# Up-projection weight sums moved from VectorE to GpSimd, read from a second copy of the weight, and two layouts in DRAM changed

## The chip, the cores and the metric

One core of a Trainium2 chip runs the whole program. The metric is the device time of one execution in microseconds (us). The engines are named as in the profile: PE is TensorE (with PEld, its weight loads), DVE is VectorE, ACT is ScalarE, POOL is GpSimd, and SP is SyncE, which does nothing here but issue DMAs, one after the other, from one queue in program order.

## What is computed

One layer of a streaming encoder over 2048 prompt tokens and 64 sample tokens, all in float32: a modulated RMSNorm, one input projection that feeds a pooling mixer and an mLSTM with 4 heads, an output projection, then a second modulated norm and a gated MLP with a causal convolution of width 3. The part that the change touches belongs to the MLP:

```
up = h2 @ w_up                      # (tokens, 1024) @ (1024, 5632)
conv = b_conv + sum(w_conv[j] * upp[:, j:j + T] for j in range(3))
a, g = split(conv, 2)
x = x + gt2 * ((silu(g) * a) @ w_down)
```

## The kernel before

**Number format.** A float32 matrix product is made of three passes: each operand is kept as a high part and a low part (ACT copies to the high part, line 411; DVE subtracts to get the low one, line 414; together a "split"), and high x high, high x low and low x high are added in PSUM. A split weight block is a tile `wt` of 128 partitions x 2 x 512; there are 7 such buffers. A block that comes unsplit from DRAM lands in a `raw` tile first.

**Stages.** Attention runs in 4 groups g of 512 tokens (the last one of 576), up to about 800 us of the span. In each, PE walks through the projections (line 1117 for `v`, line 477 for q, k, the output gate, the pooling input and the output projection). The mLSTM of a head is made of small pieces of work between these matmuls: `GL` (a copy of decays from PSUM to SBUF on DVE), `kw` (the keys times decays, DVE, from PE's transposes on line 1282), the state update `st`, `SP` (DVE, from PE's line 1307), the outputs `nd` (DVE), and a scale `sf` and a row scale `RS`, whose power of -0.5 POOL takes (lines 1349 and 545). The MLP then runs in 3 groups of 704 tokens (line 1572 is the up-projection).

**Up-projection with seven products.** The weight of the up-projection is cut into 22 blocks f. Per block, Strassen's scheme needs 7 products: three of them (lines of `up_unit`) use pieces of `w_up` itself, the other four (`sum_unit`) use sums and differences of its four pieces a0, a1, g0, g1. These four sums are worked out while attention groups 1 to 3 run, by the generator `up_sums` (lines 843 to 872), and kept in DRAM (`wsum`). There are 44 items: 22 blocks times two halves of 256 columns. An item is a load of a tile `w` (4 x 256 columns, two DMAs, four buffers `w4`), four additions or subtractions on DVE (lines 863, 864, 866, 867), and a store. Loads are made three items ahead. The generator is moved on by one step at four places of each projection row (`tick(4)` in `gemm`), and its instructions are pinned to keep their order among themselves. The MLP's first group reads all four sums from `wsum`, splits them and keeps three of them split in `wsplit`; the later two groups read those three split and the fourth from `wsum` again.

**Kept split weights.** In attention group 0 the q, k, gate and pooling weights are split once and kept in DRAM (`hl_kept`, 32 blocks, line 419 stores), and groups 1 to 3 load them from there (line 395). Their last axis is 528 long, of which 512 are used.

**Another user of DVE and SP.** In groups 1 to 3 the generator `ada` makes more modulation vectors: for 16 steps i = 0 to 15, a load of `raw` from `w_ada` (line 194) and two multiply-adds on DVE (line 210; line 208 for the first of each half). These too sit in DVE's and SP's order between the other work.

**What sets the order.** A scheduler orders each engine's instructions at build time, and on the chip every engine runs its list in order. Waits are on semaphores, so an instruction that waits holds back all behind it on its engine or queue. A DMA also waits for the one eight places before it, which used the same semaphore. A `w4` buffer can be loaded again only when the store from it has landed.

Of the kernel before, what the change touches and what calls it, by code (L numbers as in the profile page):

```python
# [9 lines left out]
F32 = mybir.dt.float32  # L10
F32R = mybir.dt.float32r
AF = mybir.ActivationFunctionType
ALU = mybir.AluOpType
# [3 lines left out]
P = 128  # L17
D = 1024
KD = D // P
# [5 lines left out]
NF = 22  # L25
# [17 lines left out]
WN = 2 * 264  # L43
# [19 lines left out]

@with_exitstack
def tile_layer(ctx: ExitStack, tc: tile.TileContext, xT, vecs, cst, rst, w_mod, w_ada, w_qkou, w_v, w_pool,
               w_out, w_up, w_down, w_quad, st_C, st_pool, yT, o_pool, o_C, o_m, o_conv):
    nc = tc.nc
    act, dve, pool, pe = nc.scalar, nc.vector, nc.gpsimd, nc.tensor

# [12 lines left out]
    dr = ctx.enter_context(tc.tile_pool(name="dr", bufs=1, space=DRAM))  # L82
# [17 lines left out]
    def scr():  # L100
        return sp.tile([P, TMAX], F32, tag="scr", name="scr")


    bg = ([], [], [], [], [])
# [152 lines left out]
    for g in range(NG):  # L257
# [20 lines left out]
    OUT, INSIDE, WHOLE = range(3)  # L278
    stream = []

    hl_kept = dr.tile([32, P, 2, WN], F32, tag="hl_kept", name="hl_kept")
    place_of = {}

    def halves(key, src, n):
# [39 lines left out]

    def sum_unit(g, f, i):
        if i not in KEPT:
            return (wsum[f, :, i], 512, INSIDE, None)
        kept = wsplit[f, KEPT.index(i)]
        return (kept, 512, WHOLE, None) if g else (wsum[f, :, i], 512, INSIDE, kept)

    dsum = dr.tile([8, P, 4, 512], F32, tag="dsum", name="dsum")

    def quad_units(p, first):

        out = []
        for d in (2 * p, 2 * p + 1):
            raw, sums = [[(t[d, :, i], 512, place, None) for i in range(4)] for t, place in ((w_quad, OUT), (dsum, INSIDE))]
# [35 lines left out]
    class Unit:  # L373

        state = 0
        w = raw = None
# [7 lines left out]
    def issue():  # L384
        u = Unit()
        src, u.n, place, u.keep, u.stays = stream[pos[0]] + (OUT, None, False)[len(stream[pos[0]]) - 2:]
        u.at = pos[0]
        if place == OUT:
            u.raw = raw_tile()
            nc.sync.dma_start(out=u.raw[:, :u.n], in_=src)  # L390
        else:
            u.w = wt_tile(u.n)
            if place == WHOLE:
                u.state = 2
                nc.sync.dma_start(out=u.w.bitcast(F32)[:, :, :u.n], in_=src)
            else:
                u.raw = u.w.bitcast(F32)[:, 1]
                nc.sync.dma_start(out=u.raw[:, :u.n], in_=src)
        pos[0] += 1
        pend.append(u)  # L400

# [269 lines left out]
    class Sums:  # L671
# [165 lines left out]
    if True:  # L837
# [3 lines left out]
        C = a1.tile([P, NCST], F32, tag="C", name="C")  # L841
        RST = a1.tile([4, TMAX], F32, tag="RST", name="RST")

        def up_sums():

            def load(f, c):
                w = a1.tile([P, 4, 256], F32, tag="w4", name="w4", bufs=4)
                for i in range(2):
                    tc.keep_in_program_order(nc.sync.dma_start(out=w[:, 2 * i:2 * i + 2, :], in_=w_up[NF * i + f].rearrange(
                        "p (h c) -> p h c", h=2)[:, :, c:c + 256]))  # L850
                return w
            todo = [(f, c) for f in range(NF) for c in (0, 256)]
            pin = tc.keep_in_program_order
            nx = [load(*todo[i]) for i in range(3)]
            yield
            yield
            for i, (f, c) in enumerate(todo):
                w = nx.pop(0)
                yield
                yield  # L860

                a0, a1_, g0, g1 = (w[:, i, :] for i in range(4))
                pin(dve.tensor_tensor(out=g1, in0=g0, in1=g1, op=ALU.add))
# [3 lines left out]
                pin(dve.tensor_tensor(out=a1_, in0=a1_, in1=a0, op=ALU.subtract))  # L867
                yield

                if i + 3 < len(todo):  # L870
                    nx.append(load(*todo[i + 3]))
                pin(nc.sync.dma_start(out=wsum[f, :, :, c:c + 256], in_=w))

        def fold():

# [92 lines left out]
        h, pb, pr0 = [], [], []  # L968
# [462 lines left out]
        for o in groups:  # L1431
            drain(1)
            if o.g == 1:
                bg[4].append(up_sums())
            if o.g > 0:
                bg[3].append(ada(2 + o.g, False))
            if o.g == 0:
# [10 lines left out]
            if o.g == 0:  # L1448
                t = scr()
# [11 lines left out]
            for hd in range(NH):  # L1461
# [38 lines left out]
            h = hn  # L1500
# [14 lines left out]
    todo = []  # L1515
# [149 lines left out]
    class Pair:  # L1665
# [115 lines left out]
        def blocks(self):  # L1781
            return [self.of(i)[:, j * FH:(j + 1) * FH] for i in range(1 + self.second) for j in (0, 1)]
# [306 lines left out]
    for o in fgroups:  # L2089
        Bo = B[o.g]  # L2090
        held = None
        for pi, part in enumerate(PARTS[o.g]):
# [99 lines left out]
            for secs in [(c,) for c in ENDS] if ends else (ENDS,):  # L2192
                sums = [(ssum, 0)]
# [98 lines left out]
```

## Time and profile before

| what | value |
|---|---|
| time, median of 3 runs | 2187.92 us (2184.07 to 2188.07) |
| span of the profiled execution, first to last instruction | 2178.0 us |
| between the median and that span | 9.92 us |
| PE busy in the span | 2155.1 us (99%) |
| DVE busy | 1631.7 us (75%) |
| ACT busy | 1093.7 us (50%) |
| POOL busy | 241.6 us (11%) |
| moved by DMA | 539.51 MB in 297351 packets |

The time of the profiled execution itself is not listed beside its span; the runs listed differ from the span by what lies around the first and the last instruction, and the prediction takes that part as unchanged. "Busy" counts an engine's instructions while they run; for PE the ends of matmuls are modelled, so short waits can hide inside them. A row of a group of instructions has line, engine, operation, output and inputs, shapes, the count, then the busy time, the mean duration of one in ns, and the idle time just before them with what ended it. A timeline row has start, length, engine, line and tile, and in brackets the idle time before it and what ended that.

### The profile page before, as it was taken

The numbers are of one execution on the slowest core, as the hardware profiler recorded it, in microseconds if no ns is written. First come the engines' busy times: TensorE is split into PE (matmuls) and PEld (weight loads), VectorE is DVE, ScalarE is ACT, GpSimd is POOL, SyncE is SP. The second block draws the span as 40 slices with busy tenths as digits, with TensorE's granted clock in tenths as the row PEclk, the third lists the DMA queues.
The fourth block names the chain that finished last, engine by engine and source line by source line (L and its number), as shares of the span: only waits on it lengthen the run. The fifth ranks groups of instructions, "written<-read, shape, count | busy, mean of one in ns | idle before, by whom it ended". The sixth has DMA issues, their size and how long they took to land.

```text
span 2178.0 us, 38112 instructions
## 1 busy us (share of the span) xinstructions
PE 2155.1 (99%) x13553; PEld 2041.6 (94%) x13553; DVE 1631.7 (75%) x3040; ACT 1093.7 (50%) x2181; POOL 241.6 (11%) x474
## 2 busy tenths in 40 slices
PE   8999999999999999999999999999999999999998
PEld 7888888888899999999999999999999999999998
DVE  5868668757955678797967668888886587887874
ACT  4554335234333456474736445655655364565554
POOL 0010000001000101010101121100101331111112
PEclk9999999999999999999999999999999999999999
DMA  8886997988879387788967966666668675555542
GB/s 325 327 297 226 312 312 259 310 291 273 296 263 305 130 279 255 267 306 295 349 211 257 316 244 225 237 201 215 227 220 275 217 255 183 170 179 190 172 161 81
DMA packets 297351, 539.51 MB, mean 248 GB/s; under 512 B 25760, under 2 KB 114336, under 8 KB 297160
## 3 DMA queue, kind: packets, MB, share of 16 engines
q1 hardware_dynamic: 287720, 514.75, 69.8%
q10 hardware_dynamic: 9440, 22.32, 2.6%
q8 instruction: 107, 1.75, 0.3%
q14 instruction: 84, 0.69, 0.1%
HBM read 410.98 MB, written 125.98 MB: 247 GB/s over the span
## 4 chain that ended last, share of the span: by engine, by line
PE 82%; DMA 7%; DVE 7%; issue 2%; ACT 1%; SPq 1%; POOL 0%; DVEq 0%; POOLq 0%; ACTq 0%
PE mm L1572 35%; PE mm L477 19%; PE mm L2138 12%; PE mm L2015 8%; PE mm L1117 2%; DVE wt L414 2%; DMA raw<-w_ada 1%; DMA wt<-wsum 1%; DMA hl_kept<-wt 1%; DMA wsum<-w 1%; PE m L1307 1%; PE m L1329 1%; PE m L1327 1%; PE m L1292 1%; DVE scr L250 1%
## 5 line engine op out<-in xcount | busy, mean ns | idle before, releaser
L1572 PE MATMUL mm<-hx,wt 128*128 128x352 f32 x5544 | 887.0, 321 | 3.7 <-DVE hx L768 1.9
L1572 PEld LDWEIGHTS mm<-hx,wt 128*128 128x128 f32 x5544 | 878.6, 188 | 6.8 <-DVE hx L768 2.8
L477 PE MATMUL mm<-hl,wt 128*128 128x512 f32 (+2 forms) x1920 | 386.2, 357 | 0.2 <-ACT va L250 0.2
L411 ACT ACTIVATE wt<-raw 128x512 fp32r<-128x512 f32 (+3 forms) x470 | 276.8, 597 | 185.2 <-PE mm L477 63.5
L477 PEld LDWEIGHTS mm<-hl,wt 128*128 128x128 f32 x1920 | 315.4, 189 | 48.2 <-issue 5.3
L414 DVE TENSOR_TENSOR wt<-raw,wt 128x512 fp32r<-128x512 f32 (+3 forms) x470 | 312.2, 670 | 53.2 <-ACT wt L411 52.7
L2138 PE MATMUL mm<-av,wt 128*128 128x448 f32 (+1 forms) x1632 | 262.7, 322 | 0.0
L2138 PEld LDWEIGHTS mm<-av,wt 128*128 128x128 f32 x1632 | 250.4, 188 | 11.1
L1987 DVE SCALAR_TENSOR_TENSOR x<-mm,MOD,x 128x352 f32<-128x352 f32 (+3 forms) x360 | 167.2, 503 | 79.2 <-PE mm L2138 65.7
L2015 PE MATMUL mm<-av,wt 128*128 128x352 f32 x1344 | 220.6, 323 | 1.8 <-DVE x L1987 0.7
L2015 PEld LDWEIGHTS mm<-av,wt 128*128 128x128 f32 x1344 | 215.4, 188 | 4.8 <-DVE ea L1581 2.8
L1619 ACT ACTIVATE mm<-mm 128x352 f32<-128x352 f32 x196 | 87.8, 448 | 240.0 <-PE mm L1572 184.0
L477 PE MATMUL mm<-mx,wt 128*128 128x512 f32 (+1 forms) x960 | 182.6, 352 | 0.0
L477 PEld LDWEIGHTS mm<-mx,wt 128*128 128x128 f32 x960 | 159.3, 188 | 22.5
L1550 DVE SCALAR_TENSOR_TENSOR ta<-ea,V,ta 128x704 f32<-128x704 f32 (+1 forms) x132 | 125.6, 952 | 63.2 <-ACT ta L1545 51.2
L1550 DVE SCALAR_TENSOR_TENSOR tg<-eg,V,tg 128x704 f32<-128x704 f32 (+1 forms) x132 | 125.7, 952 | 61.0 <-ACT tg L1545 58.5
L414 DVE TENSOR_TENSOR wt<-wt 128x512 fp32r<-128x512 f32 x196 | 132.7, 683 | 12.8 <-ACT wt L411 12.7
L411 ACT ACTIVATE wt<-wt 128x512 fp32r<-128x512 f32 x196 | 119.2, 622 | 43.1 <-DMA wt<-wsum 40.1
L1759 ACT ACTIVATE tg<-tg 128x704 f32<-128x704 f32 (+1 forms) x66 | 52.5, 795 | 70.5 <-DVE tg L1550 70.5
L1528 POOL COPY ea<-UC 128x2 f32<-128x2 f32 x66 | 32.8, 497 | 482.6 <-DVE ta L1550 394.0
L1117 PE MATMUL mm<-wt,hl 128*128 128x256 f32 (+1 forms) x576 | 71.3, 284 | 0.0
L1117 PEld LDWEIGHTS mm<-wt,hl 128*128 128x128 f32 x576 | 70.4, 190 | 0.8 <-issue 0.6
(304 smaller groups left out, 2188.2 us busy)
## 6 DMA issues: line engine op xcount, KB each, us to landing
wt<-wsplit SPq DMA_DIRECT2D x132, 512.0 KB, 4.2
raw<-w_up SPq DMA_DIRECT2D x198, 256.0 KB, 3.8
wt<-hl_kept SPq DMA_DIRECT2D x96, 512.0 KB, 6.0
wt<-wsum SPq DMA_DIRECT2D x132, 256.0 KB, 5.3
wsplit<-wt SPq DMA_DIRECT2D x66, 512.0 KB, 5.5
w<-w_up SPq DMA_DIRECT2D x88, 256.0 KB, 3.7
wsum<-w SPq DMA_DIRECT2D x44, 512.0 KB, 4.9
Bd<-fscr ACTq DMA_DIRECT2D x56, 352.0 KB, 4.3
```

The costliest lines, as they stand in the source:

```text
L411: act.activation(u.w[:, 0, :u.n], u.raw[:, :u.n], AF.Copy)
L414: dve.tensor_tensor(out=u.w[:, 1, :u.n], in0=u.raw[:, :u.n], in1=u.w[:, 0, :u.n].bitcast(F32), op=ALU.subtract)
L477: pe.matmul(ps[bi][:, :hi - lo], U[:, a, k % 4 * P:(k % 4 + 1) * P], mv[k][:, b, lo:hi], start=(at == 0 and pi == 0), stop=(k == order[-1] ...
L1117: pe.matmul(ps[ti][:n, :cols], h[4 * kh + k4][:, b, lo:lo + n], U[:, a, k4 % 2 * cols:(k4 % 2 + 1) * cols], start=(kh == 0 and k4 == 0 and ...
L1528: pool.tensor_copy(ext[:, 0:2], UC[:, f, :])
L1550: dve.scalar_tensor_tensor(out=t[:, :E], in0=ext[:, j:j + E], scalar=wc(j, f), in1=t[:, :E], op0=ALU.mult, op1=ALU.add)
L1572: pe.matmul(bk.t[:, :FH], U[:, a, kc * P:(kc + 1) * P], Bo.at(nm, kc, b), start=(first and kc == 0 and pi == 0), stop=(kc == 3 and pi == 2 ...
L1619: act.activation(to.t[:, :FH], bk.t[:, :FH], AF.Copy)
L1759: act.activation(self.tg[:, :E], self.tg[:, :E], AF.Silu)
L1987: dve.scalar_tensor_tensor(out=x3[n][:, a:b], in0=bk.t[:, a - lo:b - lo], scalar=gt2(n, s), in1=x3[n][:, a:b], op0=ALU.mult, op1=ALU.add)
L2015: pe.matmul(bk.t[:, :FH], U[:, a, c:c + P], quad.put(op, m, b), start=(first and m == 0 and pi == 0), stop=(m == 1 and pi == 2), skip_grou ...
L2138: pe.matmul(bks[i].t[:, :hi - lo], U[:, a, k % 4 * P:(k % 4 + 1) * P], av[k][:, b, lo:hi], start=(k == 0 and (a, b) == PASSES[0]), stop=(k ...
```

## The change

Four things change.

1. `up_sums` becomes `weight_sums`: the four operations of an item go to POOL (lines 867, 868, 872, 873 of the new file) instead of DVE.
2. Their input is a second copy of `w_up`, `w_sums`, which is made on the host and holds an item's four pieces side by side, 4 KB for each partition: one DMA per item instead of two. The result array `wsums` has the same layout, 4 KB per partition. The MLP reads one sum of a block out of it in two pieces of 1 KB per partition instead of one of 2 KB.
3. The store of an item is written after the first two operations of the next item. The load three items ahead then goes into a buffer whose store stands two steps before it.
4. `hl_kept` loses its padding (528 to 512), so that a partition's high and low halves are 4 KB in one piece.

```diff
-    hl_kept = dr.tile([32, P, 2, WN], F32, tag="hl_kept", name="hl_kept")
+    hl_kept = dr.tile([32, P, 2, 512], F32, tag="hl_kept", name="hl_kept")
...
-    wsum = dr.tile([NF, P, 4, 512], F32, tag="wsum", name="wsum")
+    wsums = dr.tile([NF, 2, P, 4, 256], F32, tag="wsums", name="wsums")
+
+    def sum_of(f, i):
+        return wsums[f, :, :, i].rearrange("j p c -> p j c")
...
-            return (wsum[f, :, i], 512, INSIDE, None)
+            return (sum_of(f, i), 512, INSIDE, None)
...
-        def up_sums():
-
-            def load(f, c):
-                w = a1.tile([P, 4, 256], F32, tag="w4", name="w4", bufs=4)
-                for i in range(2):
-                    tc.keep_in_program_order(nc.sync.dma_start(out=w[:, 2 * i:2 * i + 2, :], in_=w_up[NF * i + f].rearrange(
-                        "p (h c) -> p h c", h=2)[:, :, c:c + 256]))
-                return w
...
-                pin(dve.tensor_tensor(out=g1, in0=g0, in1=g1, op=ALU.add))
-                pin(dve.tensor_tensor(out=g0, in0=a0, in1=g0, op=ALU.subtract))
-                yield
-                pin(dve.tensor_tensor(out=a0, in0=g1, in1=a0, op=ALU.subtract))
-                pin(dve.tensor_tensor(out=a1_, in0=a1_, in1=a0, op=ALU.subtract))
-                yield
-
-                if i + 3 < len(todo):
-                    nx.append(load(*todo[i + 3]))
-                pin(nc.sync.dma_start(out=wsum[f, :, :, c:c + 256], in_=w))
+        def weight_sums():
+
+            pin = tc.keep_in_program_order
+            todo = [(f, j) for f in range(NF) for j in (0, 1)]
+
+            def load():
+                if not todo:
+                    return None
+                f, j = todo.pop(0)
+                w = a1.tile([P, 4, 256], F32, tag="w4", name="w4", bufs=4)
+                pin(nc.sync.dma_start(out=w, in_=w_sums[f, j]))
+                return wsums[f, j], w
+            nx = [load() for _ in range(3)]
+            yield
+            yield
+            before = None
+            while nx[0]:
+                to, w = nx.pop(0)
+                a11, a12, a21, a22 = (w[:, i] for i in range(4))
+                pin(pool.tensor_tensor(out=a22, in0=a21, in1=a22, op=ALU.add))
+                pin(pool.tensor_tensor(out=a21, in0=a11, in1=a21, op=ALU.subtract))
+                if before:
+                    pin(nc.sync.dma_start(out=before[0], in_=before[1]))
+                yield
+                pin(pool.tensor_tensor(out=a11, in0=a22, in1=a11, op=ALU.subtract))
+                pin(pool.tensor_tensor(out=a12, in0=a12, in1=a11, op=ALU.subtract))
+                before = to, w
+                yield
+                nx.append(load())
+                yield
+                yield
+            pin(nc.sync.dma_start(out=before[0], in_=before[1]))
```

PE's list of instructions is the same in both programs, row for row. The lists of DVE, POOL and SP change as follows at the three places that matter below; in names such as `w_4463` the number tells one buffer's use from another.

DVE at the start of group 3, before: the copies `CL`, the row scale `RS`, two whole items of sums, then `GL` and `kw` of the first head.

```order
L543 TENSOR_SCALAR RS_121<-m_6567 128x4
L863 TENSOR_TENSOR w_6153<-w_6153 128x256
L714 TENSOR_TENSOR scr<-scr 128x352
L864 TENSOR_TENSOR w_6153<-w_6153 128x256
L866 TENSOR_TENSOR w_6153<-w_6153 128x256
L867 TENSOR_TENSOR w_6153<-w_6153 128x256
L863 TENSOR_TENSOR w_6595<-w_6595 128x256
L864 TENSOR_TENSOR w_6595<-w_6595 128x256
L866 TENSOR_TENSOR w_6595<-w_6595 128x256
L867 TENSOR_TENSOR w_6595<-w_6595 128x256
L250 COPY GL<-m_6621 128x20
```

DVE at the same place now:

```order
L547 TENSOR_SCALAR RS_121<-m_6536 128x4
L718 TENSOR_TENSOR scr<-scr 128x352
L250 COPY GL<-m_6589 128x20
L250 TENSOR_TENSOR at<-at,mask 128x512
L250 TENSOR_TENSOR at<-at,mask 64x64
```

Nothing that waits for a load stands ahead of `GL` any more.

POOL at the start of group 2, before: the power for `RS` and the first `sf`, with nothing between them.

```order
L1391 COPY UH<-u 128x16
L1381 COPY u<-UH 128x16
L1391 COPY UH<-u 128x16
L545 TENSOR_TENSOR RS_121<-RS_121,half 128x4
L1349 TENSOR_TENSOR sf<-sf,half 128x4 x2
```

POOL there now: items 18 (`w_4463`) and 19 (`w_4511`) stand behind `RS`, which waits for DVE, and ahead of `sf`.

```order
L549 TENSOR_TENSOR RS_121<-RS_121,half 128x4
L867 TENSOR_TENSOR w_4463<-w_4463 128x256
L868 TENSOR_TENSOR w_4463<-w_4463 128x256
L872 TENSOR_TENSOR w_4463<-w_4463 128x256
L873 TENSOR_TENSOR w_4463<-w_4463 128x256
L867 TENSOR_TENSOR w_4511<-w_4511 128x256
L868 TENSOR_TENSOR w_4511<-w_4511 128x256
L872 TENSOR_TENSOR w_4511<-w_4511 128x256
L873 TENSOR_TENSOR w_4511<-w_4511 128x256
L1356 TENSOR_TENSOR sf<-sf,half 128x4
```

So items 18 and 19 cannot begin before DVE has made `RS` and POOL has taken its power.

SP at the same place in group 2, before; the last three single loads from `w_ada` are steps i = 13, 14 and 15 of `ada`, and one store of sums stands among them.

```order
L194 DMA raw<-w_ada 128x512 x3
L395 DMA wt<-hl_kept 128x2x512 x2
L194 DMA raw<-w_ada 128x512
L395 DMA wt<-hl_kept 128x2x512
L194 DMA raw<-w_ada 128x512
L395 DMA wt<-hl_kept 128x2x512
L872 DMA wsum<-w_3872 512x1x256
L395 DMA wt<-hl_kept 128x2x512
L194 DMA raw<-w_ada 128x512
```

SP there now; the first two single loads from `w_ada` are steps 12 and 13, and the pair is steps 14 and 15.

```order
L194 DMA raw<-w_ada 128x512
L870 DMA wsums<-w_4463 128x1024
L194 DMA raw<-w_ada 128x512
L399 DMA wt<-hl_kept 128x1024
L858 DMA w_4742<-w_sums 128x1024
L399 DMA wt<-hl_kept 128x1024
L870 DMA wsums<-w_4511 128x1024
L194 DMA raw<-w_ada 128x512 x2
L399 DMA wt<-hl_kept 128x1024
```

The load of step 13 now stands behind the store of item 18, and those of steps 14 and 15 behind the store of item 19; both stores wait for the POOL operations shown above. On DVE the two multiply-adds of step 13 (line 210) now stand between `GL` and `kw` of group 2's first head, where they stood ahead of `GL`.

More of the change, by code (lines that the diff above doesn't have):

```diff
@@ L65, in tile_layer @@
 def tile_layer(ctx: ExitStack, tc: tile.TileContext, xT, vecs, cst, rst, w_mod, w_ada, w_qkou, w_v, w_pool,
-               w_out, w_up, w_down, w_quad, st_C, st_pool, yT, o_pool, o_C, o_m, o_conv):
+               w_out, w_up, w_down, w_quad, w_sums, st_C, st_pool, yT, o_pool, o_C, o_m, o_conv):
     nc = tc.nc
@@ L326, in sum_unit @@
         if i not in KEPT:
-            return (wsum[f, :, i], 512, INSIDE, None)
+            return (sum_of(f, i), 512, INSIDE, None)
         kept = wsplit[f, KEPT.index(i)]
-        return (kept, 512, WHOLE, None) if g else (wsum[f, :, i], 512, INSIDE, kept)
+        return (kept, 512, WHOLE, None) if g else (sum_of(f, i), 512, INSIDE, kept)
     dsum = dr.tile([8, P, 4, 512], F32, tag="dsum", name="dsum")
@@ L336, in quad_units @@
         for d in (2 * p, 2 * p + 1):
-            raw, sums = [[(t[d, :, i], 512, place, None) for i in range(4)] for t, place in ((w_quad, OUT), (dsum, INSIDE))]
+            raw, sums = [[(t[d, :, i], 512, place, None) for i in range(4)] for t, place in ((w_quad, OUT), (dsum.rearrange("d p i (j c) -> d p i j c", j=2), INSIDE))]
             out += [raw[0], sums[WS1]] + first + [raw[1], sums[WS2], sums[WS3], sums[WS4], raw[3]]
@@ L397, in issue @@
                 u.raw = u.w.bitcast(F32)[:, 1]
-                nc.sync.dma_start(out=u.raw[:, :u.n], in_=src)
+                nc.sync.dma_start(out=u.raw[:, :u.n].rearrange("p (j c) -> p j c", j=2), in_=src)
         pos[0] += 1
@@ L855, in up_sums @@
             yield
             yield
-            for i, (f, c) in enumerate(todo):
-                w = nx.pop(0)
+            before = None
[12 more added lines that the diff above has]
+                nx.append(load())
@@ L859, in up_sums @@
                 yield
                 yield
-                a0, a1_, g0, g1 = (w[:, i, :] for i in range(4))
-                pin(dve.tensor_tensor(out=g1, in0=g0, in1=g1, op=ALU.add))
-                pin(dve.tensor_tensor(out=g0, in0=a0, in1=g0, op=ALU.subtract))
-                yield
-                pin(dve.tensor_tensor(out=a0, in0=g1, in1=a0, op=ALU.subtract))
-                pin(dve.tensor_tensor(out=a1_, in0=a1_, in1=a0, op=ALU.subtract))
-                yield
-                if i + 3 < len(todo):
-                    nx.append(load(*todo[i + 3]))
@@ L1433, in tile_layer @@
             if o.g == 1:
-                bg[4].append(up_sums())
+                bg[4].append(weight_sums())
             if o.g > 0:
@@ L2246 @@
     w_quad = six.transpose(4, 1, 3, 0, 6, 2, 5, 7).reshape(8, P, 4, 512)
+    w_up = blocks(i["w_up"][0], KD)
+    w_sums = w_up.reshape(2, NF, P, 2, 2, 256).transpose(1, 4, 2, 0, 3, 5).reshape(NF, 2, P, 4, 256)
     arrays = {
@@ L2262 @@
         "w_out": blocks(i["w_out"][0], KD),
-        "w_up": blocks(i["w_up"][0], KD),
+        "w_up": w_up,
         "w_down": w_down,
         "w_quad": w_quad,
+        "w_sums": w_sums,
         "st_C": np.concatenate([i["state_mlstm_C"][0, 0].transpose(2, 0, 1),
```

3 lines of the change are left out of this document (removed).

## The prediction

> **What bounds the kernel now.** I read the page's busy times first, then the same by stretches of the span. Whole span:
>
> ```profile
> span 2178.0 us, 38112 instructions
> PE 2155.1 (99%) x13553; PEld 2041.6 (94%) x13553; DVE 1631.7 (75%) x3040; ACT 1093.7 (50%) x2181; POOL 241.6 (11%) x474
> ```
>
> Busy time by stretch; the columns are start and end, length, PE, PEld, DVE, ACT and POOL with their counts, granted clock, DMA share, GB/s:
>
> ```profile
> 0.00:165.00 165.00, 156.35 (x1120) 132.68 (x1121) 113.22 (x231) 84.35 (x193) 12.39 (x26) 1.00 0.86 313
> 165.00:905.00 740.00, 736.81 (x4509) 661.88 (x4508) 538.12 (x1108) 311.32 (x711) 49.16 (x85) 1.00 0.80 267
> 905.00:2178.00 1273.00, 1261.90 (x7928) 1247.00 (x7926) 980.37 (x1702) 698.01 (x1277) 180.01 (x363) 1.00 0.67 228
> ```
>
> The sums are worked out between 165 and 905 us. There PE idles 740.00 - 736.81 = 3.19 us, the granted clock is 1.00, and PE's list does not change. So PE's waits are all that can shrink, and DVE's and POOL's loads count only where PE waits for them. Next view, PE's waits in that stretch (what waited, for what, total us, count, mean):
>
> ```profile
> PE mm L1572 <- DVE hx L768: 1.9, 3, 0.8
> PE m L1282 <- DVE GL L250: 1.0, 1, 1.0
> PE m L1307 <- DVE kw L250: 0.2, 1, 0.2
> ```
>
> These three are 3.1 of the 3.19 us. The hx waits come where attention ends and the MLP begins, the GL wait at the start of group 3, the kw wait at a group's first head.
>
> **The change, part by part.** The arithmetic and the transfers it moves:
>
> ```profile
> L863 DVE TENSOR_TENSOR w<-w 128x256 f32<-128x256 f32 x44 | 18.3, 416 | 10.6 <-DMA w<-w_up 8.7 <-issue 1.8
> L867 DVE TENSOR_TENSOR w<-w 128x256 f32<-128x256 f32 x44 | 18.4, 419 | 0.7
> L1979 POOL TENSOR_TENSOR ssum<-ssum,fscr 128x256 f32<-128x256 f32 x4 | 2.9, 736 | 8.8 <-ACT fscr L1978 8.8
> ...
> raw<-w_up SPq DMA_DIRECT2D x198, 256.0 KB, 3.8
> ...
> w<-w_up SPq DMA_DIRECT2D x88, 256.0 KB, 3.7
> wsum<-w SPq DMA_DIRECT2D x44, 512.0 KB, 4.9
> ```
>
> DVE loses 4 x 44 = 176 operations of about 0.418 us, 73.6 us, and 10.6 us of waits for `w_up` at their head. All of it lies beside PE work except where the three waits above end. POOL gains 176 x 0.736 = 129.5 us (its own same-shaped operation) on 49.16 busy of 740: a quarter, hidden as long as nobody waits for an item.
>
> *Group 3's start, a gain.* DVE there stood in front of two items before it came to GL:
>
> ```profile
> 628.25 0.42 DVE L863 TENSOR_TENSOR w<-w 128x256 f32<-128x256 f32 x1 [5.77 <-DMA w<-w_up]
> ...
> 629.97 0.17 DVE L250 COPY GL<-m 128x20 f32<-128x20 f32 x1
> 630.19 0.30 PE L1282 MATMUL m<-V,k 128*64 128x128 f32 x1 [1.03 <-DVE GL L250]
> ```
>
> With the items gone from DVE's list GL needs no load: PE's 1.03 us goes. **-1.0** (bounds -1.0 and 0). Late next is `kw` of that head.
>
> *Into the MLP, a gain.* The chain of waits runs here through the last store and a load queued behind it:
>
> ```profile
> 758.43 5.40 DMA wsum<-w
> 763.91 3.18 DMA fscr<-h2d
> ```
>
> The last items will be done on POOL before DVE reaches them today, so this store can leave earlier, but `h2d` itself comes from DVE. Of the 1.9 us of hx waits I take a third, **-0.6** (bounds -1.9 and 0).
>
> *Group 2's start, a loss.* This is where work is now chained that was not. Today:
>
> ```profile
> 419.67 0.55 SPq L194 DMA_DIRECT2D raw<-w_ada  x1
> 430.21 0.27 PE L538 MATMUL m<-V,scr 128*128 128x128 f32 x1
> 431.93 1.20 SPq L849 DMA_DIRECT2D w<-w_up  x2
> 432.40 0.14 DVE L543 TENSOR_SCALAR RS<-m 128x4 f32<-128x4 f32 x1
> 432.62 1.01 POOL L545 TENSOR_TENSOR RS<-RS,half 128x4 f32<-128x4 f32 x1 [79.47 <-DVE RS L543]
> ...
> 438.68 0.69 DVE L250 TENSOR_TENSOR kw<-m,CL 128x512 f32<-128x512 f32 x1 [2.82 <-PE m L1282]
> 440.00 1.05 PE L1307 MATMUL m<-va,kw 128*128 128x129 f32 x8
> ```
>
> ```profile
> L210 DVE SCALAR_TENSOR_TENSOR s<-raw,CA,s 128x512 f32<-128x512 f32 x42 | 31.2, 744 | 14.3 <-DMA raw<-w_ada 14.3
> ...
> raw<-w_ada SPq DMA_DIRECT2D x48, 256.0 KB, 4.7
> ```
>
> The load of step 13 left at 419.67. Now it stands on SP behind item 18's store, that store behind four POOL operations, and those behind POOL's RS, whose input PE ends at 430.48. RS on POOL therefore ends between 431.6 (DVE takes it up at once) and 433.6 (as today). Add 4 x 0.736 = 2.9 for the item, 0.6 for the store's issue (half of the pair at 431.93), 3.7 to 4.7 until the load lands (the `w_up` and the `w_ada` medians), 2 x 0.744 for step 13's multiply-adds, which now stand between GL and kw, and 0.69 for kw. The kw ends between 441.0 and 444.0; today it ends at 439.37 and PE takes it at 440.00. PE would stall 1.0 to 4.0 us; DVE is freer, so RS is nearer its early bound: **+2.0** (bounds 0, if PE's records hide slack, and +4). Also behind that store on SP stand weight loads for PE and item 22's load; what these loads have in hand is below.
>
> *Group 3, a second such wait.* In DVE's list stands
>
> ```profile
> 681.70 0.58 DVE L731 SCALAR_TENSOR_TENSOR mx<-mx,G,mx 128x352 f32<-128x352 f32 x1 [5.52 <-DMA mx<-x2d]
> ...
> 691.81 0.34 DVE L250 SCALAR_TENSOR_TENSOR st<-SP,GL,m 128x129 f32<-128x129 f32 x1
> ```
>
> The load of `mx` now comes on SP behind three stores that wait for POOL, 3 x 2.9 = 8.8 us of items. DVE could be held to about 690 or 692, and behind it is `st`, the state update, at 691.81. **+0.5** (bounds 0 and +3), nearer nothing, because PE did not wait behind the 5.52 us of today.
>
> *SP and the weight loads.* SP issues 44 DMAs fewer, and its waits change owner:
>
> ```profile
> SPq L849 <- DMA wsum<-w: 97.1, 36, 5.9
> SPq L872 <- DVE w L867: 19.1, 13, 3.3
> ```
>
> Today 97.1 us go to loads that wait for the landing of the store from the same buffer; with the store two steps ahead of the load, part of that stays. The 19.1 us of stores waiting for DVE become stores waiting for POOL. Everything in program order behind them, the split weights above all, is late by as much. No row has PE waiting for a weight tile in this stretch while SP spent these 116 us, so this costs **0** (up to +1 inside group 2, where the held stores come in a row).
>
> *Layouts.*
>
> ```profile
> wt<-wsplit SPq DMA_DIRECT2D x132, 512.0 KB, 4.2
> ...
> wt<-hl_kept SPq DMA_DIRECT2D x96, 512.0 KB, 6.0
> wt<-wsum SPq DMA_DIRECT2D x132, 256.0 KB, 5.3
> ...
> hl_kept<-wt SPq DMA_DIRECT2D x32, 512.0 KB, 7.4
> ...
> wsplit<-wt SPq DMA_DIRECT2D x66, 512.0 KB, 5.5
> ```
>
> Unpadded, `hl_kept` should move as the 512 KB of `wsplit` do: loads 6.0 to about 4.2, stores 7.4 to 5.5. PE does not wait for these loads, so **0** (bounds -0.5 and 0). The 132 reads of sums become pieces of 1 KB instead of 2; `w<-w_up` has 1 KB pieces and lands in 3.7, `raw<-w_up` 2 KB pieces and 3.8, so **0** (up to +1).
>
> The sum: -1.0 - 0.6 + 2.0 + 0.5 = +0.9 us on PE's path. The profiled execution's span plus the 9.92 us around it is the median of the runs, 2187.9; so **2188.8 us**. The bounds added up are -3.4 (of which no more than 3.19 can be had in this stretch) and +9.
>
> **The rivals.** A change of under 0.2% (4.4 us) is about what a measurement of this kernel cannot tell from none. *Hidden anyway*, 2187.9: every loss above fits into slack that the records do not show, and the gains are too small to see; it differs from my forecast by size alone. *Slower by the loop store, POOL, SP, load*: +5 to +10, 2193 to 2198. The place is groups 2 and 3 above; if steps 14 and 15, behind item 19's store (2.9 later), also stand ahead of work that PE needs, and weight loads in hand run out, each further held store costs up to 2.9. It decides from two such stores on: 2.0 + 2.9 is past 4.4. For it: SP already waited for 19.1 us in 13 stores. Against it: PE has not waited for a weight once, and `ada` has no due time before the MLP except through DVE's order.
>
> *Slower by DVE and POOL in each other's way*:
>
> ```profile
> 1240.45 1.70 POOL L1979 TENSOR_TENSOR ssum<-ssum,fscr 128x704 f32<-128x704 f32 x1 [2.38 <-ACT fscr L1978]
> 1240.86 1.84 DVE L414 TENSOR_TENSOR wt<-raw,wt 128x512 fp32r<-128x512 f32 x1 [1.05 <-ACT wt L411]
> ...
> L414 DVE TENSOR_TENSOR wt<-raw,wt 128x512 fp32r<-128x512 f32 (+3 forms) x470 | 312.2, 670 | 53.2 <-ACT wt L411 52.7
> ```
>
> A subtraction that began inside a POOL operation took 1.84 instead of 0.67 us: DVE waited for POOL's end. So each of 176 new POOL operations can hold DVE by up to 0.736. Twelve heads of groups 1 to 3 have a kw; the one above has 440.00 - 439.37 = 0.63 us in hand. One operation ahead of each: 12 x (0.736 - 0.63) = +1.3; two: 12 x (1.47 - 0.63) = +10.1, 2198. It decides when DVE is held for over a microsecond ahead of the same kw. Against it: 176 x 0.418 us less on DVE, and kw itself reads one operand from PSUM. The Trainium skill states this as a rule ("SBUF — State Buffer", "Who interferes with whom"): a DVE instruction with two SBUF inputs contends with a GpSimd instruction that reads SBUF, and the second to issue fully blocks. The 1.84 us agrees with that; by the rule the splits of weights and POOL's sums would shut each other out throughout, which speaks against this move, and it would give the +1.3 to +10.1 just worked out instead of 0.
>
> *Faster*: all 3.19 us of waits go and nothing takes their place, 2184.7. That is still within 0.2%; for more, the 8.65 us of idle PE before 165 us, where stores of 7.4 us get shorter, would have to shrink too.
>
> **How the numbers follow.** My forecast and hidden anyway, with the 3.19 us gain: 0.72. The loop: 0.11, the lock: 0.07, together 0.18 slower by over 0.2%. Faster by over 0.2%: 0.10, the first stretch and the scatter of the runs (2184.07 to 2188.07). The range runs from 2182, the best case less the runs' scatter, to 2197, within the two slower cases.
>
> **What the profile after would show.** Right: no wait for GL at group 3's start; RS on POOL at 431 to 433 in group 2, the store of item 18 issued near 435, step 13's load after it, and PE waiting 1 to 4 us for kw; POOL busy near 179 us in this stretch at 0.74 us for one; DVE near 464; loads of `hl_kept` near 4.2. Wrong: PE waits for `wt` in groups 1 to 3 (the loop), POOL operations or splits well over their means together with waits for kw (the lock), or a PE busy time that differs, by which my floor would fall.

## The result, and the profile after

The changed kernel takes 2200.7 us (median of 4 runs, 2198.1 to 2204.3), beside 2185.99 us for the kernel before in the same comparison: a ratio of 1.0078, 95% interval 1.0060 to 1.0096. It is slower, by 14.7 us, and outside the range that was forecast.

The two profiled executions lie further apart than the medians: 2178.0 and 2202.5 us of span, 24.5 us. The one of after took 2204.3 us, the longest of its four runs, and only 1.8 us of that lie outside its span; the 9.92 us that the prediction put around the span of before were too many. What follows tells where the 24.5 us are; the medians hold some three fifths of it.

The page after, its first two lines:

```profile
span 2202.5 us, 38256 instructions
PE 2164.6 (98%) x13553; PEld 2049.3 (93%) x13553; DVE 1611.8 (73%) x2864; ACT 1092.9 (50%) x2181; POOL 400.8 (18%) x650
```

PE's busy time rose by 9.5 us (2164.6 against 2155.1) with the same 13553 matmuls, and its idle time by 15.0 us (37.9 against 22.9). DVE was to lose 73.6 us and lost 19.9. The stretch from 165 to 905 us (columns as in the prediction), and the longest of PE's waits in it. The numbers of a wait are the total, the count and the longest one; the prediction calls this last number a mean:

```profile
165.00:905.00 740.00, 720.30 (x4357) 643.41 (x4357) 500.42 (x898) 302.23 (x698) 207.38 (x261) 0.99 0.76 260
```

```profile
PE m L1314 <- DVE kw L250: 7.0, 2, 5.9
PE mm L1124 <- DVE scr L250: 3.5, 2, 3.0
PE m L1334 <- DVE st L250: 3.4, 1, 3.4
PE mm L481 <- ACT k L1242: 2.2, 1, 2.2
PE mm L1579 <- DVE hx L772: 1.1, 2, 0.6
```

PE idles 19.7 us here, where it idled 3.19. The wait for GL is gone and the one for hx shorter, as forecast; kw was 0.2 us before, and st, scr and k are new. The same three places of the timeline that the prediction spoke of (start, length, engine, line, tile). Group 2, with the store of item 18 and the load of step 13 on SP:

```profile
436.25 1.02 POOL L549 TENSOR_TENSOR RS<-RS,half 128x4 f32<-128x4 f32 x1 [27.46 <-DVE RS L547]
437.24 0.74 POOL L867 TENSOR_TENSOR w<-w 128x256 f32<-128x256 f32 x1
...
439.67 1.05 POOL L873 TENSOR_TENSOR w<-w 128x256 f32<-128x256 f32 x1
...
440.75 0.33 SPq L870 DMA_DIRECT2D wsums<-w  x1
441.13 0.42 SPq L194 DMA_DIRECT2D raw<-w_ada  x1
...
445.28 0.75 DVE L210 SCALAR_TENSOR_TENSOR s<-raw,CA,s 128x512 f32<-128x512 f32 x1 [3.92 <-DMA raw<-w_ada]
...
446.61 0.68 DVE L250 TENSOR_TENSOR kw<-m,CL 128x512 f32<-128x512 f32 x1
447.44 2.06 PE L1314 MATMUL m<-va,kw 128*128 128x129 f32 x8 [5.92 <-DVE kw L250]
```

The chain is the one described, link by link: RS on POOL, the item, its store, the load behind the store, the multiply-adds, kw, PE. It starts later and its item takes longer than was priced. Group 3:

```profile
699.28 6.85 SPq L870 DMA_DIRECT2D wsums<-w  x3
...
709.20 0.58 SPq L748 DMA_DIRECT2D mx<-x2d  x1
...
717.45 0.58 DVE L735 SCALAR_TENSOR_TENSOR mx<-mx,G,mx 128x352 f32<-128x352 f32 x1 [6.49 <-DMA mx<-x2d]
...
719.02 0.49 PE L1334 MATMUL m<-st,q 128*128 128x129 f32 x2 [3.43 <-DVE st L250]
```

Three stores wait for POOL, the load of `mx` leaves only at 709.20, DVE waits for it, and PE for `st` behind it. And just before, DVE and POOL beside each other, with what waits for them:

```profile
694.39 2.48 DVE L250 TENSOR_TENSOR nd<-nd,sf 128x512 f32<-128x512 f32 x2 [0.81 <-POOL sf L1356]
...
695.66 1.07 POOL L868 TENSOR_TENSOR w<-w 128x256 f32<-128x256 f32 x1
696.80 1.06 DVE L735 SCALAR_TENSOR_TENSOR mx<-mx,G,mx 128x352 f32<-128x352 f32 x2
696.80 1.65 POOL L872 TENSOR_TENSOR w<-w 128x256 f32<-128x256 f32 x1
697.40 1.08 ACT L738 ACTIVATE mx<-mx,MOD 128x352 f32<-128x352 f32 x2 [3.77 <-DVE mx L735]
698.39 0.69 ACT L1242 ACTIVATE k<-mm 128x256 f32<-128x256 f32 x2
...
698.81 2.52 PE L481 MATMUL mm<-hl,wt 128*128 128x256 f32 x12 [2.25 <-ACT k L1242]
```

The two `nd` operations took 0.89 us together at the same place before; now they take 2.48, and POOL's operations beside them and the `mx` behind them up to 1.65, where 0.74 is what one takes alone. ACT waits for that `mx`, its copy of `k` stands behind, and PE waits 2.25 us for `k`: the 1.6 us by which the `nd` are longer reach PE over ACT's list, with no store in between. Last, the stretches around two of PE's waits (columns as in the prediction's stretches; the granted clock is the third number from the end):

```profile
440.00:450.00 10.00, 4.08 (x21) 3.54 (x20) 5.47 (x11) 0.52 (x3) 4.03 (x5) 0.71 0.83 262
450.00:460.00 10.00, 10.00 (x51) 8.42 (x51) 5.24 (x14) 4.38 (x16) 1.61 (x2) 0.95 0.92 337
690.00:700.00 10.00, 7.75 (x57) 7.38 (x56) 6.53 (x17) 5.79 (x24) 6.38 (x7) 1.00 0.42 137
700.00:710.00 10.00, 10.00 (x51) 8.86 (x50) 3.42 (x6) 2.04 (x7) 5.37 (x7) 0.66 0.61 216
```

Around these waits the clock falls: a mean of 0.71 and 0.66 over 10 us, where it was 1.00 in the same stretches before. Taken microsecond by microsecond it is 0.50 from 445 to 451 and from 701 to 707 us, and 0.60 in the one ahead of each. PE's work there takes longer, which is in the 9.5 us of busy time.

### The profile page after: what moved, and what is told of

Read it like the earlier page. It is cut to its first block, busy times and chain, and to the rows that moved or that the text cites. A ratio compares the mean times of both kernels' runs of the same rounds, so it can differ in the third digit from the quotient of the medians.

```text
span 2202.5 us, 38256 instructions
## 1 busy us (share of the span) xinstructions
PE 2164.6 (98%) x13553; PEld 2049.3 (93%) x13553; DVE 1611.8 (73%) x2864; ACT 1092.9 (50%) x2181; POOL 400.8 (18%) x650
## 4 chain that ended last, share of the span: by engine, by line
PE 76%; DMA 9%; DVE 9%; issue 3%; ACT 2%; SPq 1%; POOL 0%; DVEq 0%; POOLq 0%; ACTq 0%
PE mm L1579 34%; PE mm L481 15%; PE mm L2145 12%; PE mm L2022 8%; DVE wt L418 2%; DMA wsums<-w 2%; DMA raw<-w_ada 2%; DMA wt<-wsums 1%; PE mm L1124 1%; DMA mx<-x2d 1%; DVE scr L250 1%; PE m L1314 1%; PE m L1334 1%; PE m L1336 1%; PE m L1299 1%
```

## The experiments

Three theories stood at first. A, the loop: stores on SP wait for POOL, loads behind them come late to DVE, and PE waits for DVE (the prediction's second rival). B, the lock: DVE and POOL hold each other while POOL reads SBUF (its third). C: the layouts or the later store, whatever the engine.

**sums_on_dve.** The changed kernel with the four operations on DVE.

```diff
-                pin(pool.tensor_tensor(out=a22, in0=a21, in1=a22, op=ALU.add))
+                pin(dve.tensor_tensor(out=a22, in0=a21, in1=a22, op=ALU.add))
...
```

> The changed kernel with its four operations of an item on DVE again; layouts, loads, packets and the later store stay. Theory A (the loop: a store on SP waits for POOL, and loads from w_ada and x2d behind it come late to DVE, so PE waits) and rival B (the lock: DVE and POOL hold each other at SBUF) both expect the loss gone: 2183 to 2189 us, PE waits between 430 and 765 us of at most 4 us in all, no stretch with a granted clock under 1 before the end. Rival C (it is the layout, or the store an item later, that upsets SP's order, whatever the engine): 2197 to 2203, with the waits for kw and st still there.

Measured: 2179.46 us against 2182.4, ratio 0.9981 (0.9967 to 0.9994). C falls: layouts and the later store cost nothing. The whole loss hangs on the engine. One point of the expectation was missed: the clock did fall once, at 262 us, at a kw wait of 2.4 us.

**only_pool.** The kernel before with the four operations on POOL and nothing else.

```diff
-                pin(dve.tensor_tensor(out=g1, in0=g0, in1=g1, op=ALU.add))
+                pin(pool.tensor_tensor(out=g1, in0=g0, in1=g1, op=ALU.add))
...
```

> The kernel before with one edit: the four operations of an item on POOL; two loads of w_up, the old layouts, and the store right behind its item as before. A: the store on SP now stands closer behind the POOL operations that it waits for than in the changed kernel, so at least as slow: 2196 to 2215. B: about as the changed kernel, 2196 to 2204, with no more waiting on SP. C: no change, 2184 to 2189.

Measured: 2214.49 us, ratio 1.0144 (1.0127 to 1.0161). The move alone costs more than the whole change, within A's range and over B's; what the rest of the change did was to give some of that back.

**store_by_pool.** The changed kernel, stores issued by POOL.

```diff
-                    pin(nc.sync.dma_start(out=before[0], in_=before[1]))
+                    pin(nc.gpsimd.dma_start(out=before[0], in_=before[1]))
...
```

> The changed kernel, its sums on POOL, but the store of an item issued from POOL's own queue instead of SP's, so that nothing on SP waits for POOL. A: the 67.9 us of SP's waits for POOL go, the kw wait (5.9 us) and the st wait (3.4 us) go, 2183 to 2190 us. B: POOL and DVE are as busy together as in the changed kernel, so 2196 to 2204. If the issue from POOL costs it a microsecond or more for each of 44 stores, POOL's items come later, which A alone doesn't mind.

Measured: 2189.5 us, ratio 1.0024 (1.0011 to 1.0038): at the upper end of A's range, under B's, and with a loss left that is clear of the scatter. The kw and st waits of groups 2 and 3 are gone, but PE waits for DVE in other places:

```profile
PE mm L1124 <- DVE scr L250: 5.3, 2, 4.1
PE mm L481 <- DVE scr L250: 2.4, 2, 2.1
PE m L1336 <- DVE at L250: 2.0, 1, 2.0
```

Taking SP's waits for POOL away gives back 0.54 of the 0.78%; something else keeps the rest. The scheduler also ordered DVE's and SP's lists differently here in many places, so this is not the changed kernel less one thing.

**only_unpad.** The kernel before with `hl_kept` unpadded.

```diff
-    hl_kept = dr.tile([32, P, 2, WN], F32, tag="hl_kept", name="hl_kept")
+    hl_kept = dr.tile([32, P, 2, 512], F32, tag="hl_kept", name="hl_kept")
```

> The kernel before with one edit: the kept split weights without padding in DRAM. A, B: no change in time, 2183 to 2188, since PE doesn't wait for these loads; loads of wt from hl_kept land sooner than the 6.0 us of before, and stores sooner than 7.4. C: if this layout is what harms, over 2192. The opposite of C, if DMA contention counts: under 2182.

Measured: ratio 1.0007 (0.9995 to 1.0019). No change. Its stores land in 6.4 us instead of 7.4, its loads in 5.9 instead of 6.0.

**pool_writes_only.** Fills with zeros in place of the sums, which are left out.

```diff
-                pin(pool.tensor_tensor(out=a22, in0=a21, in1=a22, op=ALU.add))
+                pin(pool.memset(w[:, 1:], 0.0))
...
```

> The changed kernel with the four operations of an item replaced by four fills of three quarters of the same tile with zeros on POOL, about 0.74 us each as the operations were: POOL's time, the stores that wait for it and SP's order stay as they are, but POOL reads nothing from SBUF. The sums are left out (the up-projection's four summed products are of zeros). Theory A (the loop over SP) expects most of the loss to stay: the kw wait of 4 to 6 us and the st wait of 2 to 4 us, 2192 to 2201 us. Rival B (the lock on SBUF reads) expects 2180 to 2186. If both act, as the run with stores from POOL's queue suggests (it kept 5.3 us of the 14 to 18), the time lies 4 to 6 us under the changed kernel and the wait for scr near 590 us is gone, while kw and st stay.

Measured: 2176.99 us, ratio 0.9973 (0.9960 to 0.9986). Nothing of the loss is left, against A's expectation, and DVE's busy time for the same 2864 instructions fell to 1573.4 us from 1611.8. SP still waited 45.6 us for POOL (67.9 in the changed kernel), but the scheduler had put step 13's load ahead of item 18's store here, so at that place the loop was not tested.

**both_gone.** Fills, and stores from POOL's queue.

> Both edits together: stores from POOL's own queue and fills in place of the sums on POOL (sums left out). If the loop and the lock are all there is, nothing of the loss is left: 2177 to 2184 us, PE waits of at most 4 us between 165 and 905 us. If a third cause is at work (the layouts, the loads of 1 KB pieces, the order of ada's multiply-adds on DVE), it stays over 2186.

Measured: 2177.75 us, ratio 0.9976 (0.9965 to 0.9986). With neither loop nor lock nothing is lost, so no third cause of loss shows. This kernel and the one with fills alone multiply zeros in the MLP, but that stage is not faster for it: from the start of its first up-projection matmul to that of its last it takes 1325.6 and 1326.3 us, and 1325.7 in store_by_pool, where the sums are made.

**store_2_later.** Stores one item later still, loads two ahead.

```diff
-            nx = [load() for _ in range(3)]
+            nx = [load() for _ in range(2)]
...
-                if before:
-                    pin(nc.sync.dma_start(out=before[0], in_=before[1]))
+                if len(late) == 2:
+                    o, t = late.pop(0)
+                    pin(nc.sync.dma_start(out=o, in_=t))
...
```

> The changed kernel with the store two items later instead of one, still on SP, and for that the loads two ahead instead of three, since there are four buffers. A: SP seldom waits for POOL any more (67.9 us to under 20), kw and st waits mostly go, 2186 to 2194, like the run with stores from POOL's queue; but loads may now wait longer for the landing of stores, and if these waits take the place of the others on SP, it stays at 2195 to 2205. B: 2196 to 2204 whatever SP does.

Measured: 2195.29 us, ratio 1.0051 (1.0035 to 1.0068). SP still waits 31.5 us for POOL, and one st wait of 6.3 us appeared. A later store shrinks the loop, and does not end it. The time lies at the edge of both theories' ranges and decides nothing between them.

**kw_x10.** The kernel before with one head's kw written ten times.

```diff
+                for _ in range(10 if o.g == 2 and hd == 0 else 1):
```

> The kernel before with one edit: kw of the first head of group 2 is written ten times over, nine times 0.69 = 6.2 us more DVE work ahead of one PE instruction that had 0.63 us in hand, so PE waits 5 to 6 us once, as in the changed kernel's group 2. It measures what one such wait costs at the end. If a wait costs only its own length: +5 to +6 us. If the granted clock drops to half for about 7 us behind it, as the changed kernel's windows from 444 to 451 us show: +7 to +10 us. If the later work takes the delay up again: under +4.

Measured: 2182.4 us, ratio 0.9996 (0.9981 to 1.0011). A miss as an experiment: the scheduler ordered PE's list anew, with the matmuls that use this kw behind a block of 24 others, so PE waited 0.8 us there. What one wait costs with its clock was not measured this way.

**fill_256 and fill_strided.** Fills of 256 elements, next to each other or every fourth.

```diff
-                pin(pool.tensor_tensor(out=a22, in0=a21, in1=a22, op=ALU.add))
+                pin(pool.memset(flat[:, 3], 0.0))     # flat: "p i (c s) -> p s (i c)", s=4
...
```

> The changed kernel with fills of 256 elements in place of the four operations on POOL (sums left out). Unlike the fills of 768, these leave the order of every engine and of SP as it is in the changed kernel, but for three swaps of neighbours that nothing waits for: the load of step 13 stands behind item 18's store again, which it did not in the run with 768. POOL reads nothing, so no lock; an item takes about 1.2 us of POOL instead of 3.6. The loop alone, by the rows of the changed kernel: RS on POOL to 433.6, item to 434.8, store and load issued by 435.5, landed by 439.5, two multiply-adds and kw to 441.7 against 440.0: PE waits 1 to 3 us for kw in group 2; 2176 to 2182 us in all. If the loop needs no lock, the waits for kw (over 4) and st (over 2) are there again: 2186 to 2196.

> As the run with fills of 256, but every fourth element of the tile is filled instead of neighbours, in case that makes a fill slower on POOL without the lock and without a change of order. If a fill then takes near 0.74 us: as the loop alone with its full POOL time, 1 to 4 us of kw wait in group 2, 2177 to 2184. If not, a second measurement of fill_256.

Measured: 0.9988 (0.9976 to 1.0001) and 1.0006 (0.9994 to 1.0018). A strided fill took 0.56 to 0.62 us, so an item took 2.2 us in group 2, short of the 2.9 us of the prediction. The orders are those of the changed kernel but for a few neighbours, step 13 behind the store included. This is the loop alone, with shorter items:

```profile
435.85 0.33 SPq L870 DMA_DIRECT2D wsums<-w  x1
436.22 0.42 SPq L194 DMA_DIRECT2D raw<-w_ada  x1
```

```profile
PE m L1314 <- DVE kw L250: 3.1, 2, 2.1
PE m L1334 <- DVE st L250: 0.6, 1, 0.6
PE mm L1579 <- DVE hx L772: 0.4, 1, 0.4
```

The kw wait in group 2 is 2.1 us and the one for st 0.6: what the prediction had put there (2.0 and 0.5). At its two places the loop alone costs PE what was forecast. That the ratio of 1.0006 is also that of the forecast, 1.0004 (2188.8 to 2187.92), is in part luck: with neither loop nor lock the kernel stood at 0.9976, a larger gain than the 1.6 us (0.07%) of the forecast, so that the loop would have to cost more than 2.5 us too.

**sums_on_dve_5 and dve_at_once.** The first is sums_on_dve with more rounds, the second has the store back at its old place.

> The kernel with the new layouts and the later store, sums on DVE, again with more rounds: 0.9975 to 0.999 of the kernel before if its gain (0.9981 [0.9967, 0.9994]) is real, 1.000 if it was the scatter of runs.

> The same with the store of an item written right behind the item's operations, as in the kernel before: new layouts alone, on DVE. If the later store brings the gain: 1.000; if the layouts (44 fewer loads on SP, whole packets) bring it: 0.9975 to 0.999, like the other.

Measured: 0.9989 (0.9978 to 0.9999) and 0.9996 (0.9985 to 1.0007). The first beats the kernel before by 0.1 to 0.2% in both measurements. The two means lean to the later store as what brings it, but their intervals overlap, and it is not shown.

**idle_reads and idle_fills.** What stayed open was whether POOL's reads cost anything when nobody waits for the operations that make them. Both start from the kernel before, with sums on DVE, and add work on POOL that nothing uses; the lists of the other engines and of SP are unchanged.

```diff
+            dum = a1.tile([P, 256], F32, tag="dum", name="dum")
...
+                pin(pool.tensor_tensor(out=dum, in0=dum, in1=dum, op=ALU.mult))
+                pin(pool.tensor_tensor(out=dum, in0=dum, in1=dum, op=ALU.mult))
```

> The kernel before with one addition: between the four operations of an item on DVE, four multiplications of 128x256 on POOL, from and to a tile of its own that nothing else uses (176 in all). The lists of PE, DVE, ACT and SP are the same row for row; nothing waits for these operations except POOL's own later ones. So no loop over SP can act. If the lock alone costs time: DVE's busy time rises by 30 to 50 us for the same instructions (in the changed kernel 1611.8 against 1573 with fills), and the time by 5 to 15 us, since DVE has the sums as well. If the lock only harms through the loop: 1.000 of the kernel before, whatever DVE's busy time.

> The same addition with fills of 128x768 (0.74 us each) in place of the multiplications: as much POOL time ahead of POOL's sf and RS, but no reads. If the reads are what costs: DVE's busy time stays at 1631 to 1634 and the time at 0.999 to 1.001. If it is POOL's queue (sf and RS come later behind the items), it is as slow as the one with reads.

Measured: 1.0086 (1.0071 to 1.0101), 2201.53 us, with reads, and 1.0000 (0.9988 to 1.0013) with fills. The second line of each page, reads first:

```profile
PE 2163.6 (98%) x13553; PEld 2050.4 (93%) x13553; DVE 1678.1 (76%) x3040; ACT 1093.6 (50%) x2181; POOL 379.4 (17%) x651
```

```profile
PE 2158.4 (99%) x13553; PEld 2044.7 (94%) x13553; DVE 1632.7 (75%) x3040; ACT 1094.2 (50%) x2181; POOL 373.0 (17%) x651
```

176 reading operations on POOL make DVE's 3040 instructions 45.4 us longer, 0.26 us for each; as many fills of the same length, nothing. And PE waits for DVE, with reads:

```profile
PE mm L1123 <- DVE scr L250: 9.9, 3, 4.0
PE m L1313 <- DVE kw L250: 4.3, 2, 3.2
PE m L1288 <- DVE GL L250: 2.8, 1, 2.8
```

This is B by itself: no loop through POOL, no changed order, no wait for the added operations, and a loss as large as the change's. DVE has the sums here as well, so it is fuller than in the changed kernel, and the size does not carry over to it.

## Why the prediction was wrong

*What held.* The GL wait at group 3's start went (-1.0). The hx waits went from 1.9 to 1.1 us (-0.8; -0.6 was said). PE never waited for a weight tile between 165 and 905 us, and no run shows a cost of the reads in pieces of 1 KB. Both losing places were named with their mechanism, and with the lock out of the way they measured 2.1 and 0.6 us against 2.0 and 0.5, with items of 2.2 us instead of 2.9. The layouts' landing times were forecast wrong, at no cost: `hl_kept` loads took 6.8 us instead of 4.2, its stores 6.2 instead of 5.5.

*The step that failed* is the lock's, DVE and POOL in each other's way: it stands at nothing in the sum, was priced as a rival at the twelve kw heads alone, and was given 0.07. The price took the 0.63 us in hand at one head and asked whether one or two POOL operations fit. It should have been DVE's whole list made longer. In the changed kernel DVE's time for 2864 instructions is 1611.8 us against 1573.1 in the run of strided fills, 38.7 us or 0.22 for each POOL operation. The 73.6 us that DVE was to be freed of were too many themselves: records of DVE operations in a row overlap (in the kernel before, sums of 0.42 us begin 0.33 apart at 401 us), and without the lock its busy time falls by 58.6 us, 0.33 for each. Two thirds of that came back. Three groups of DVE between 165 and 765 us, before and after:

```profile
L578 DVE SCALAR_TENSOR_TENSOR scr<-hl,G,rb 128x512 f32<-128x512 f32 x24 | 17.7, 743 | 0.0
L581 DVE SCALAR_TENSOR_TENSOR hl<-scr,MOD,hl 128x512 fp32r<-128x512 f32 x24 | 17.8, 746 | 1.3 <-ACT hl L580 1.2
L250 DVE SCALAR_TENSOR_TENSOR scr<-mm,MOD,scr 128x512 f32<-128x512 f32 x24 | 17.9, 746 | 7.4 <-PE mm L477 7.2
```

```profile
L582 DVE SCALAR_TENSOR_TENSOR scr<-hl,G,rb 128x512 f32<-128x512 f32 x24 | 20.6, 863 | 0.0
L585 DVE SCALAR_TENSOR_TENSOR hl<-scr,MOD,hl 128x512 fp32r<-128x512 f32 x24 | 19.9, 828 | 3.2 <-ACT hl L584 3.1
L250 DVE SCALAR_TENSOR_TENSOR scr<-mm,MOD,scr 128x512 f32<-128x512 f32 x24 | 17.9, 745 | 5.3 <-PE mm L481 5.1
```

The first two read two tiles of SBUF and became longer; the third has the same shape, reads one of its two tiles, `mm`, from PSUM, and did not.

The argument against that rival, that DVE loses 176 x 0.418 us of work, looked at the mean of the stretch. DVE is not evenly loaded: before the change it is busy 19.50 and 19.96 of 20 us from 520 to 560 us, and a list that is full there cannot be made longer without being late behind it. The waits for scr between 587 and 599 us follow on it (3.0 us in the changed kernel, 4.1 with stores from POOL, 4.0 with idle reads; none in the run of strided fills). DVE also waits for loads from `w_ada` between 500 and 600 us, but no longer than before: 4.4 us before, 3.6 now.

*A second step failed,* the sizes of the loop's terms. RS on POOL was bounded to end by 433.6 and ended at 437.27; the item was put at 2.9 us and took 3.45; the rest of the chain kept its estimates (load issued to first use 4.15 us, within 3.7 to 4.7). The kw wait came to 5.9 us instead of 2.0, and the one for st to 3.4 instead of 0.5. The 0.736 us for a POOL operation was a row from a stretch where it ran beside little on DVE; in this stretch one takes 0.88 to 0.92 on average. The late RS is the largest part of the excess, and its bound had left out what stands ahead of it on DVE: the multiply-adds of steps 10 and 11, which wait for a load. In the changed kernel, and in the run of strided fills:

```profile
433.27 0.75 DVE L210 SCALAR_TENSOR_TENSOR s<-raw,CA,s 128x512 f32<-128x512 f32 x1 [6.56 <-DMA raw<-w_ada]
```

```profile
429.68 0.75 DVE L210 SCALAR_TENSOR_TENSOR s<-raw,CA,s 128x512 f32<-128x512 f32 x1 [4.87 <-DMA raw<-w_ada]
```

RS follows on DVE at 436.01 and 432.42 us, 2.74 us behind in both, so the 3.6 us between the two runs are all that load's. SP issued it 1.0 us later (423.22 against 422.26); why it also landed later is open, and so is how much of this is the lock's.

*A term was missing:* the clock. Behind some waits PE does not go on at full speed. PE's busy time is 9.5 us longer for the same list, beside 15.0 us more idle time: two fifths of the difference between the two profiled executions. Up to the first matmul of the MLP it is 7.5 us longer (791.1 against 783.7); the rest arises behind the change. Of the two stretches of some 7 us at half clock, PE stood waiting in the first until 447.44 us, so it cost about 1.8 us of its work, and the second about 3.4: by this estimate 5 of the 7.5. What the others are is open. The forecast counted waits one for one; a PE busy time that differs was among its signs of being wrong.

*Two rivals at once.* By the ratios to the kernel before, with neither loop nor lock the kernel stands at 0.9976 (both_gone), with the loop alone at 1.0006 (fill_strided, its items shorter), with the lock alone at 1.0024 (store_by_pool), with both at 1.0078. Against neither, that is 0.30% for the loop, 0.48% for the lock and 1.02% for the two. With intervals of about 0.15% each way, these ratios alone do not show which counts for more, nor that the two do more together than their sum. A second reading has less scatter in it: when PE starts on the up-projection of the MLP, behind all of the sums. The kernel before, both_gone, fill_strided, store_by_pool and the changed kernel (shortest, median and longest duration in ns, then first and last start):

```profile
L1572 PE MATMUL mm<-hx,wt x5544: 317/322/435, 793.5 to 2123.1; 128*128 128x352 f32 x198
L1578 PE MATMUL mm<-hx,wt x5544: 318/322/430, 795.4 to 2121.0; 128*128 128x352 f32 x198
L1579 PE MATMUL mm<-hx,wt x5544: 318/322/430, 797.6 to 2123.3; 128*128 128x352 f32 x198
L1579 PE MATMUL mm<-hx,wt x5544: 318/322/430, 806.9 to 2132.6; 128*128 128x352 f32 x198
L1579 PE MATMUL mm<-hx,wt x5544: 317/322/431, 817.8 to 2147.3; 128*128 128x352 f32 x198
```

From the first start to the last the five take 1325.6 to 1329.6 us for the same matmuls; the first start of one program, sums_on_dve and sums_on_dve_5, is 796.7 and 795.5. Against neither, PE starts there 2.2 us later with the loop alone, 11.5 with the lock alone, and 22.4 with both. It is one execution of each, and the orders are not all the same, but it points to the lock as the larger part, to a loop that costs about what was forecast while there is no lock, and to some 9 us that only the two together cost. The forecast had them as exclusive cases with chances of their own, and its gains were set against one of them only; they act in the same places at once.

The Trainium skill's rule quoted there ("SBUF — State Buffer", "Who interferes with whom") proved the better guide than the mean load: it says that a DVE instruction with two SBUF inputs contends with a GpSimd instruction that reads SBUF, not with one that only writes it. The pair of idle reads and idle fills agrees: 46.4 us more DVE time than before against 1.0.

## What to carry to other kernels

A move of two-input arithmetic from DVE to POOL does not free DVE of that time: here each POOL operation that reads SBUF gave back 0.22 us of the 0.33 us by which it relieved DVE. Price it on DVE's fullest stretch, not on its mean, and test it cheaply by adding idle reads of the same size on POOL with every other list unchanged. A store on the queue that also carries another engine's loads hands its wait to them; and with PE at 99%, a wait of a few microseconds may cost more than its length, as the second of the two half-clock stretches did (2.25 us of wait, and about 3.4 of slower work behind it).

## What the runs showed of the hardware that was not expected

The granted clock fell to half for some 7 us around PE waits, but not by their length alone: it fell with waits of 2.25 us (1.4 us after it) and 5.92 us (while it lasted) in the changed kernel and not with those of 3.01 and 3.43 us in the same execution; with stores from POOL's queue it fell with 1.99 and 4.06. What decides it stays open.

POOL's reads slowed DVE far more than the reverse in one arrangement: with idle reads POOL's operations took 0.73 to 0.81 us on average, near their 0.74 alone, while DVE lost 45.4 us. In the changed kernel they took 0.88 to 0.92.
